# Weight products grouped by high and low parts, and block 2's merges laid out by tokens

## The chip, the cores and the metric

The kernel runs on one core of a Trainium2 chip. A core has a matrix engine, TensorE (PE in the profile, with its weight loads shown apart as PEld), a vector engine (DVE), a scalar engine (ACT), GpSimd (POOL) and SyncE (SP), which issues the transfers from HBM. Each engine works through its own queue in order, and semaphores tie the queues together. TensorE writes into PSUM, and ACT and DVE read it from there. The metric is the device time of the core in microseconds, the median of several executions.

## What is computed

Two blocks of two layers each over 256 tokens of width 1024, all in float32. A layer of block 1 mixes three branches: an mLSTM (a recurrence with gates, run forwards and backwards), a differential attention and a Fourier mix. A layer of block 2 mixes two attentions and ends in a wide MLP. Cut to what the change touches:

```
# block 1, gates of the recurrence: running sums b, running maxima, decays
b = jnp.cumsum(fc, axis=-1)
inter = b + m_st[..., None]
m_row = jnp.maximum(jnp.max(dmat, axis=-1), inter)
a = jnp.exp(dmat - m_row[..., None]) * jnp.einsum('bhtd,bhsd->bhts', qc, kc)

# block 2, one layer
proj = h @ w_in
q_a, k_a, v_a, q_b, k_b, v_b, gate_a, gate_b = jnp.split(proj, IN_OFFSETS, axis=-1)
y_a = swa_attention(q_a, k_a, v_a, sinks) @ w_o_swa
y_b = moba_attention(q_b, k_b, v_b) @ w_o_moba
mixed = jax.nn.sigmoid(gate_a) * y_a + jax.nn.sigmoid(gate_b) * y_b
x = x + gt1[:, None, :] * (mixed @ w_out)
u = jnp.square(jax.nn.relu(rms_adaln(x) @ w_up))
x = x + gt2[:, None, :] * (u @ w_down)
```

## The kernel before

**Products in three parts.** Every large product is made of three. A weight tile of 128 x 1024 comes from HBM (SP's queue, tile name w or a slot s), ACT copies it rounded into its high part (`nc.scalar.activation(h, self.raw[i], AF.Copy)` in `split`), and DVE subtracts that from the tile for the low part. The activations have a high and a low part too (h and hl, or slots). For each piece of the contraction the program makes high x high, high activations x low weights, and low activations x high weights, all added up in one PSUM bank (tiles mm).

**The stream.** `Stream.execute` (L500 on) walks through a list of gemms. A gemm of contraction 1024 has four weight tiles, numbered q = 0 to 3, each with two contraction pieces of 128 by 512 columns (kq is 2). A gemm has several outputs o. In `tok` form an output is 128 tokens by 512 features: the activations are the stationary operand and 512 weight columns move (names `mm<-w,h`). In `feat` form an output is 128 features by the tokens: the weights are stationary and the tokens move, 256 of them in block 2 (names `mm<-h,w`, 128x256). The outer loop is over q, the next over o, then over the two pieces, then over the three products; with `head` or `tail` set, the first or last tiles go output by output. `tile` (L478) hands out a tile only when both parts are planned. The first product of a tile needs its high part; the low part is needed by the second product in `tok` form and by the third in `feat` form, and PE's queue stands still until it is there.

**The order of the rest.** All other work (norms, attention, gates, evacuations) is written as generators that a `Planner` advances. It keeps a running estimate of when each engine is free. After every three products `execute` issues transfers, up to six side steps whose inputs should be there (`plan.side`), and then one `split`: the low part of the oldest tile that has a high part, or else the next high part. Nine buffers of 128 x 1024 hold raw tiles, high parts and low parts, and at most three tiles are split at a time. So the order in each engine's queue is fixed when the program is built; on the chip an engine waits where the estimate was off.

**The gates of the recurrence.** `mlstm_gates` (L1069) runs once in each layer of block 1. On rows 0 to 3 and 32 to 35 it makes the running sums and maxima, then copies the chunk ends one by one into TG, forms the maxima M and the offsets off between chunks, and with 8 and 12 small DVE instructions on 4 x 128 elements (`nc.vector.tensor_scalar(rk[k][rr, cs], R0[rr, cs], off[rr, k, j:j + 1], None, ALU.add)`) the maxima cm and three shifted copies r1, r2, r3. Five small transposes for each of four chunks turn the rows into the columns `cols`.

**Block 2's merges.** In `layer2` (L2145) four gemms in `feat` form give the two gates (`ev_g` puts tanh into tg), and four shorter ones, of contraction 512 and so of two tiles each (wo2), give the two attention outputs. `ev_o` multiplies and adds on DVE, and rounds the sum into the high and low parts yf, which already stand with features on the partitions, as the next gemm (wout2) needs them as its stationary operand. `tneed` makes wout2 wait for the eight pieces of yf one by one.

Of the kernel before, what the change touches and what calls it, by code (L numbers as in the profile page):

```python
# [11 lines left out]
ALU = mybir.AluOpType  # L12
# [37 lines left out]
NSIDE, SLACK, MAXEV, LATE = 6, 1200.0, 4, 400  # L50
NP, NJ, MP = 3, 5, 2
# [284 lines left out]
class Stream:  # L336
# [64 lines left out]
    def build_seq(self):  # L401
# [29 lines left out]
        self.nd = self.ns = self.nl = self.pairs = 0  # L431
# [20 lines left out]
    def split(self, force=False):  # L452
# [5 lines left out]
        if self.nl < self.ns:  # L458
            i = self.gidx[self.nl]
            if force or plan.gate([self.h[i]]) <= plan.t[PE]:  # L460
# [5 lines left out]
                return True  # L466
        if self.ns < len(self.gidx) and self.pairs < (NP + MP if self.more else NP) and len(self.free) > 1 + self.ns - self.nl:
# [10 lines left out]
    def tile(self, i):  # L478

        plan = self.plan  # L480
        while i not in self.l:
# [10 lines left out]
        late = plan.gate([self.h[i], self.l[i]])  # L492
# [5 lines left out]
        return self.h[i], self.l[i]  # L498

    def execute(self):  # L500
        plan, nc = self.plan, self.nc
        self.build_seq()
        nout, evs = 0, []
# [15 lines left out]
        for st in self.prog:  # L519
# [14 lines left out]
            left = [no] * nq  # L534
            ps, seen = [None] * no, [0] * no
            for q, o in visits:
# [7 lines left out]
                h, l = self.tile(i)  # L544
# [6 lines left out]
                for j in range(kq):  # L551
                    kt = q * kq + j
                    s = slice(j * st["width"], (j + 1) * st["width"])
                    for m, (L, R, O) in enumerate(outs[o](h[:, s], l[:, s], kt, ps[o])):
                        nc.tensor.matmul(O, L, R, start=(kt == 0 and m == 0), stop=(seen[o] == st["nkt"] - 1 and m == 2))
                    seen[o] += 1
                    if j == kq - 1:
                        left[q] -= 1
                        if not left[q]:
                            self.drop(self.h.pop(i))  # L560
                            self.drop(self.l.pop(i))
                            self.pairs -= 1
                            if self.joint and self.joint[0] == i:
                                self.joint.pop(0)
                        if seen[o] == st["nkt"]:
                            evac(st["cb"], o, ps[o])
                    self.dma()
                    n = 0
                    while n < NSIDE and plan.side():
                        n += 1  # L570
                    self.split()
# [11 lines left out]
def _build(tc, a, out, es):  # L583
# [377 lines left out]
    def tok(act, t, c0=0, c1=512):  # L961
        ts = slice(128 * t, 128 * t + 128)

        def f(h, l, kt, ps):
            H, L = act(kt)
            O = ps[:, 0:c1 - c0]
            return [(H[:, ts], h[:, c0:c1], O), (H[:, ts], l[:, c0:c1], O), (L[:, ts], h[:, c0:c1], O)]
        return f

    def feat(view, f0, n):  # L970
        fs = slice(128 * f0, 128 * f0 + 128)

        def f(h, l, kt, ps):
# [4 lines left out]
            return [(h[:, fs], H, O), (h[:, fs], L, O), (l[:, fs], H, O)]  # L978
# [90 lines left out]
    def mlstm_gates(rowt, l, res):  # L1069

        def gen(lane):
            pre, lf, b, v, cm, r1, r2, r3 = (rowt[:, i, :] for i in range(8))
            R = slice(0, 36)
            nc.gpsimd.memset(rowt[R, 2, :], 0.0)
            nc.gpsimd.memset(rowt[R, 4:8, :], 0.0)
# [24 lines left out]
            TG = sm.tile([128, 2, 4], F32, name="TG", tag="TG")  # L1100
            nc.vector.memset(TG, 0.0)
            for i, arr in enumerate((b, cm)):
                fw = arr[0:4].rearrange("p (c n) -> p c n", n=128)[:, :, 127]
                bw = arr[32:36].rearrange("p (c n) -> p c n", n=128)[:, :, 0]
                nc.vector.tensor_copy(TG[0:4, i, 0:2], fw[:, 1:3])
                nc.vector.tensor_copy(TG[0:4, i, 2:4], fw[:, 0:4:3])
                for p, j in POS_B.items():
                    nc.vector.tensor_copy(TG[32:36, i, j:j + 1], bw[:, p:p + 1])
            M = sm.tile([128, 4], F32, name="M", tag="M")
            nc.vector.memset(M, 0.0)  # L1110
            for j in range(3):
                nc.vector.tensor_tensor(M[R, j + 1:j + 2], M[R, j:j + 1], TG[R, 1, j:j + 1], ALU.max)
                nc.vector.tensor_tensor(M[R, j + 1:j + 2], M[R, j + 1:j + 2], TG[R, 0, j:j + 1], ALU.add)
            off = sm.tile([128, 4, 4], F32, name="off", tag="off")
            nc.vector.tensor_copy(off[R, 1, 1:4], TG[R, 0, 0:3])
            nc.vector.tensor_tensor(off[R, 2, 2:4], off[R, 1, 2:4], TG[R, 0, 0:2], ALU.add)
            nc.vector.tensor_tensor(off[R, 3, 3:4], off[R, 2, 3:4], TG[R, 0, 0:1], ALU.add)
            yield [DVE]
            dirs = ((slice(0, 4), POS_F), (slice(32, 36), POS_B))
            for rr, pos in dirs:  # L1120
# [1365 lines left out]
```

## Time and profile before

| | |
|---|---|
| median of 3 runs | 2247.6 us (2247.15 to 2248.94) |
| profiled execution, its own time | 2247.62 us |
| its span on the profile | 2245.5 us |
| PE busy | 2200.1 us, 98% |
| DVE busy | 1485.1 us, 66% |
| ACT busy | 1104.3 us, 49% |
| DVE on the low parts of w (451 instructions) | 551.5 us |
| ACT on the high parts of w (459 instructions) | 485.1 us |
| granted TensorE clock | 0.997 over the span |

Almost every instruction is issued through one helper (L318), so groups are told apart by their tiles and not by line. A busy PE is not a PE at its peak: a matmul's record lasts longer than the distance to the next one, because matmuls overlap. What a product costs is read from the distance between starts.

### The profile page before, as it was taken

How to read it: one execution, taken by the hardware profiler on the slowest of the kernel's cores; microseconds unless marked ns; L12 is line 12 of the kernel's file. 1: busy time of each engine (PE TensorE's matmuls, PEld its weight loads, DVE VectorE, ACT ScalarE, POOL GpSimd, SP SyncE). 2: the span in 40 equal slices, each digit the busy share in tenths (PEclk: the TensorE clock that was granted, in tenths of full speed). 3: DMA queues.
4: the chain of work that ended last, by engine and by line, in shares of the span. 5: the costliest groups of instructions: out<-in, count | busy, mean ns of one | idle time of the engine just before them, and what ended most of it. 6: DMA issues, size and time to landing. Idle time of an engine off the chain costs nothing. (4 is left out here: it accounts for less than half of the span.)

```text
span 2245.5 us, 33046 instructions
## 1 busy us (share of the span) xinstructions
PE 2200.1 (98%) x12312; PEld 1821.8 (81%) x12312; DVE 1485.1 (66%) x2778; ACT 1104.3 (49%) x2110; POOL 272.6 (12%) x467
## 2 busy tenths in 40 slices
PE   8999999999999999999999999999999999999999
PEld 6877888877777877877778888787898987798987
DVE  4667745457676744687886788677766656758554
ACT  4345422235565522344543466555855645666653
POOL 1013000014121000110200142003000002100000
PEclk9999999999999999999999999999999999999999
DMA  7443344353322453365675423464354564345454
GB/s 297 144 157 109 121 167 140 132 170 118 103 98 96 140 179 131 140 206 187 233 246 185 158 83 135 157 213 151 123 195 165 180 215 160 132 145 203 160 188 150
DMA packets 99905, 359.73 MB, mean 160 GB/s; under 512 B 11960, under 2 KB 12272, under 8 KB 99744
## 3 DMA queue, kind: packets, MB, share of 16 engines
q1 hardware_dynamic: 96192, 348.34, 45.3%
q0 software_dynamic: 3552, 9.28, 1.5%
q8 instruction: 97, 1.59, 0.3%
q14 instruction: 64, 0.52, 0.1%
HBM read 354.37 MB, written 3.20 MB: 159 GB/s over the span
## 5 line engine op out<-in xcount | busy, mean ns | idle before, releaser
L318 DVE TENSOR_TENSOR w<-w,w 128x1024 fp32r<-128x1024 f32 x451 | 551.5, 1223 | 394.0 <-ACT w L318 340.0
L318 ACT ACTIVATE w<-w 128x1024 fp32r<-128x1024 f32 x459 | 485.1, 1058 | 647.6 <-PE mm L318 595.4
L318 PE MATMUL mm<-h,w 128*128 128x256 f32 (+1 forms) x3280 | 665.5, 326 | 2.8 <-DVE w L318 2.3
L318 PE MATMUL mm<-w,h 128*128 128x512 f32 (+1 forms) x1972 | 597.7, 394 | 12.2 <-DVE w L318 9.0
L318 PEld LDWEIGHTS mm<-h,w 128*128 128x128 f32 x3280 | 479.6, 190 | 57.3 <-issue 9.6
L318 PEld LDWEIGHTS mm<-w,h 128*128 128x128 f32 x1972 | 357.2, 190 | 101.4 <-DVE w L318 15.5
L318 PE MATMUL mm<-w,s 128*128 128x512 f32 x1280 | 309.1, 392 | 1.2 <-DVE w L318 1.1
L318 PE MATMUL mm<-w,hl 128*128 128x512 f32 (+1 forms) x800 | 306.7, 383 | 0.0
L318 PEld LDWEIGHTS mm<-w,s 128*128 128x128 f32 x1280 | 238.4, 188 | 52.6 <-DVE w L318 3.2
L318 PE MATMUL mm<-hl,w 128*128 128x512 f32 (+1 forms) x656 | 245.8, 375 | 0.0
L318 PE MATMUL mm<-s,w 128*128 128x512 f32 (+1 forms) x960 | 182.2, 349 | 0.0
L318 PEld LDWEIGHTS mm<-w,hl 128*128 128x128 f32 x800 | 150.8, 189 | 29.9 <-DVE hl L318 0.2
L318 PEld LDWEIGHTS mm<-s,w 128*128 128x128 f32 x960 | 153.1, 190 | 23.5 <-issue 2.0
L318 DVE SCALAR_TENSOR_TENSOR acc<-w,stat,acc 128x512 f32<-128x512 f32 x192 | 143.8, 749 | 42.3 <-DMA w<-in_wada_dram 35.5
L318 PEld LDWEIGHTS mm<-hl,w 128*128 128x128 f32 x656 | 124.0, 189 | 18.7 <-issue 1.0
L318 ACT ACTIVATE s<-mm 128x512 f32<-128x512 f32 (+2 forms) x126 | 65.2, 521 | 62.8 <-PE mm L318 62.8
L318 POOL TENSOR_TENSOR qrs<-qrs,mhalf 128x8 f32<-128x8 f32 (+2 forms) x48 | 77.1, 1607 | 4.0
L318 PE MATMUL p<-s 64*128 64x256 f32 (+3 forms) x464 | 75.4, 389 | 1.4 <-DVE s L318 0.7
L318 POOL TENSOR_SCALAR ls<-ls 128x1 f32<-128x1 f32 x72 | 29.8, 414 | 344.5 <-ACT l1a L318 127.1
L318 PE MATMUL mm<-s,s 128*128 128x512 f32 x256 | 68.7, 390 | 0.0
L318 DVE TENSOR_REDUCE ls<-p 128x1 f32<-128x512 f32 (+1 forms) x96 | 52.8, 595 | 12.7 <-PE p L318 12.3
L318 ACT ACTIVATE s<-w 128x1024 fp32r<-128x1024 f32 x43 | 45.5, 1058 | 27.7 <-PE mm L318 21.0
(348 smaller groups left out, 2399.3 us busy)
## 6 DMA issues: line engine op xcount, KB each, us to landing
w<-in_win_dram SPq DMA_DIRECT2D x272, 512.0 KB, 3.3
w<-in_wada_dram SPq DMA_DIRECT2D x144, 512.0 KB, 3.5
w<-in_wmix_dram SPq DMA_DIRECT2D x64, 512.0 KB, 3.3
w<-in_wup_dram SPq DMA_DIRECT2D x64, 512.0 KB, 3.4
w<-in_wdn_dram SPq DMA_DIRECT2D x64, 512.0 KB, 3.2
w<-in_wo_dram SPq DMA_DIRECT2D x16, 512.0 KB, 3.2
w<-in_wout_dram SPq DMA_DIRECT2D x16, 512.0 KB, 3.5
s<-in_x_dram SPq DMA_DIRECT2D x4, 512.0 KB, 7.3
```

Of the source, the lines that this page charges most:

```text
L318: r = f(*a, **k)
```

## The change

**Products by parts.** In `tok` and `feat` the three products are handed out as part 0 (high x high), part 1 (low activations x high weights) and part 2 (high activations x low weights). For the inner tiles of a gemm (neither the first nor the last, with two pieces in the tile) `execute` goes through all outputs with part 0, then all with part 1, then all with part 2. The first tile of a gemm goes output by output in the order 0, 2, 1, the last one output by output in the order 0, 1, 2. The low part of a tile is asked for only ahead of part 2.

**High parts ahead.** `split` prefers the next high part to a pending low one while fewer than AHEAD = 2 tiles past the current one have theirs, and `pump`, called after every three products, may make one split ahead of the side steps as well as one behind them.

**Gates as products.** In `mlstm_gates` the chunk ends are copied four at a time, one instruction makes the maxima, and the shifted copies are gone: two products with 36 rows, one with the rows and a repeated identity and one with ones and a block of offsets on the diagonal, give all four shifts in PSUM. One small transpose is left.

**Block 2 by tokens.** The gate gemms and the wo2 gemms go from `feat` to `tok` form. `ev_o` then works on 128 tokens by 512 features, and `turned` transposes the sum back, four 128 x 128 transposes for each of the two halves of the tokens and of the features, and makes yf's high part (ACT) and low part (DVE) out of PSUM.

**Exponentials.** In the attentions of block 2 each pair of exponentials waits for the planner's ACT (`yield [ACT]`).

```diff
 NSIDE, SLACK, MAXEV, LATE = 6, 1200.0, 4, 400
+AHEAD = 2
...
-        self.nd = self.ns = self.nl = self.pairs = 0
+        self.nd = self.ns = self.nl = self.pairs = self.cur = 0
+        self.rank = {i: k for k, i in enumerate(self.gidx)}
...
-        if self.nl < self.ns:
+        if self.nl < self.ns and not (self.ns < self.cur + AHEAD and self.split_high(force)):
             i = self.gidx[self.nl]
...
+    def high(self, i):
+
+        return self.tile(i, False)[0]
...
+    def pump(self):
+
+        self.dma()
+        if self.ns < self.cur + AHEAD:
+            self.split()
+        n = 0
+        while n < NSIDE and self.plan.side():
+            n += 1
+        self.split()
...
-            visits = [(q, o) for o in range(no) for q in range(hd)]
-            visits += [(q, o) for q in range(hd, nq - tl) for o in range(no)]
-            visits += [(q, o) for o in range(no) for q in range(nq - tl, nq)]
...
+            early, late = (0, 2, 1), (0, 1, 2)
+            steps = [(q, o, early) for o in range(no) for q in range(hd)]
+            for q in range(hd, nq - tl):
+                if 0 < q < nq - 1 and kq == 2:
+                    steps += [(q, o, (p,)) for p in late for o in range(no)]
+                else:
+                    steps += [(q, o, late if q else early) for o in range(no)]
+            steps += [(q, o, late) for o in range(no) for q in range(nq - tl, nq)]
...
-                h, l = self.tile(i)
+                self.cur = max(self.cur, self.rank[i])
+                h = self.high(i)
...
-                for j in range(kq):
-                    kt = q * kq + j
-                    s = slice(j * st["width"], (j + 1) * st["width"])
-                    for m, (L, R, O) in enumerate(outs[o](h[:, s], l[:, s], kt, ps[o])):
-                        nc.tensor.matmul(O, L, R, start=(kt == 0 and m == 0), stop=(seen[o] == st["nkt"] - 1 and m == 2))
...
+                for p in parts:
+                    l = self.tile(i)[1] if p == 2 else None
+                    for j in range(kq):
+                        kt = q * kq + j
+                        s = slice(j * st["width"], (j + 1) * st["width"])
+                        L, R, O = outs[o](h[:, s], None if l is None else l[:, s], kt, ps[o])[p]
+                        nc.tensor.matmul(O, L, R, start=(seen[o] == 0), stop=(seen[o] == total - 1))
+                        seen[o] += 1
+                        since += 1
+                        if since >= 3 and seen[o] < total:
+                            since = 0
+                            self.pump()
...
-            return [(H[:, ts], h[:, c0:c1], O), (H[:, ts], l[:, c0:c1], O), (L[:, ts], h[:, c0:c1], O)]
+            return [(H[:, ts], h[:, c0:c1], O), (L[:, ts], h[:, c0:c1], O), l is not None and (H[:, ts], l[:, c0:c1], O)]
...
-            for i, arr in enumerate((b, cm)):
-                fw = arr[0:4].rearrange("p (c n) -> p c n", n=128)[:, :, 127]
...
-                for p, j in POS_B.items():
-                    nc.vector.tensor_copy(TG[32:36, i, j:j + 1], bw[:, p:p + 1])
...
+            nc.vector.tensor_copy(MP[f_, 1:3, :], by(f_, slice(0, 2)))
...
-            for rr, pos in dirs:
-                for p, j in pos.items():
-                    cs = slice(128 * p, 128 * p + 128)
-                    nc.vector.tensor_scalar(cm[rr, cs], cm[rr, cs], M[rr, j:j + 1], None, ALU.max)
...
+            nc.vector.tensor_tensor(cm4, cm4, MP[R, :, 0:1].to_broadcast([36, 4, 128]), ALU.max)
...
-                        if j >= k:
-                            cs = slice(128 * p, 128 * p + 128)
-                            nc.vector.tensor_scalar(rk[k][rr, cs], R0[rr, cs], off[rr, k, j:j + 1], None, ALU.add)
+            for c in range(4):
+                nc.vector.tensor_tensor(off[:, c], ident[R, R].unsqueeze(1).to_broadcast([36, 4, 36]),
+                                        MP[R, c, 1:5].unsqueeze(2).to_broadcast([36, 4, 36]), ALU.mult)
...
-                for i, arr in enumerate((R0, r1, r2, r3, F)):
-                    nc.tensor.transpose(ps[:, 36 * i:36 * i + 36], arr[R, 128 * p:128 * p + 128], ident[R, R])
...
+                nc.tensor.matmul(pk, R0[R, cs], ident[R, R].unsqueeze(1).to_broadcast([36, 4, 36]), start=True, stop=False)
+                nc.tensor.matmul(pk, ones[R], off[:, p], start=False, stop=True)
+                nc.tensor.transpose(ps[:, 144:180], F[R, cs], ident[R, R])
...
-                            yield []
+                            yield [ACT]
...
-                gemm(lambda q, kind=kind, c=c: win[l, 4 + 2 * kind + c, q], 8, 512,
-                     lambda: [feat(act, f, 256) for f in range(4)], ev_g, pre=pre_g if kind + c == 0 else None)
+                gemm(lambda q, kind=kind, c=c: win[l, 4 + 2 * kind + c, q], 8, 512, toks, ev_g,
+                     pre=pre_g if kind + c == 0 else None)
...
+        def turned(t, c, src):
+
+            def gen(_):
+                pt = yield Bank(src)
+                transposes(pt, src, 4)
+                yield [pt]
+                H, L = (y[:, 4 * c:4 * c + 4, 128 * t:128 * t + 128] for y in st["yf"])
+                pv = pt.rearrange("p (k n) -> p k n", k=4)
+                nc.scalar.activation(H, pv, AF.Copy, scale=0.5)
+                yield [H]
+                nc.vector.scalar_tensor_tensor(L, pv, 0.5, H.bitcast(F32), ALU.mult, ALU.subtract)
+                plan.release(pt)
+                for kt in range(4 * c, 4 * c + 4):
+                    fin(f"yfm{l}-{kt}")
+            plan.add("yfT", gen, kind="pri")
...
                     if kind:
                         yield [FREE, t]
-                        nc.vector.tensor_tensor(t, st["tg"][:, 0, kt, :], t, ALU.add)
...
+                        nc.vector.tensor_tensor(t, st["tg"][:, 0, i, cs], t, ALU.add)
+                        turned(i, c, t)
                 gemm(lambda q, kind=kind, c=c: a["wo2"][l, kind, c, q], 4, 512,
-                     lambda ov=ov: [feat(ov, f, 256) for f in range(4)], ev_o,
+                     lambda ov=ov: [tok(ov, t) for t in range(2)], ev_o,
                      need=(f"att{kind}",) if c == 0 else ())
```

PE, block 1's second layer, a `tok` gemm with four outputs, at the third tile (q is 2; mm names the bank of an output, h and hl are the high and low activations, the first w is the tile's high part and the second its low part). Before:

```order
L318 MATMUL mm_8889<-w4_8854,hl_7968 128x512
L318 MATMUL mm_8856<-w2_8907,h_7967 128x512
L318 MATMUL mm_8856<-w8_8944,h_7967 128x512
L318 MATMUL mm_8856<-w2_8907,hl_7968 128x512
...
L318 MATMUL p2_8963<-cst_80,s3_8624 128x36 x5
L318 MATMUL mm_8869<-w2_8907,h_7967 128x512
L318 MATMUL mm_8869<-w8_8944,h_7967 128x512
L318 MATMUL mm_8869<-w2_8907,hl_7968 128x512
L318 MATMUL p3_8978<-cst_80,s3_8624 128x36 x5
```

The same place now:

```order
L319 MATMUL mm_8810<-w7_8863,h_7936 128x512 x2
L319 MATMUL mm_8827<-w7_8863,h_7936 128x512
L319 MATMUL p2_8922<-cst_80,s3_8592 128x144
L319 MATMUL p2_8922<-s3_8592,one_84 128x144
L319 MATMUL p2_8922<-cst_80,s3_8592 128x36
...
L319 MATMUL mm_8849<-w7_8863,h_7936 128x512 x2
L319 MATMUL mm_8810<-w7_8863,hl_7937 128x512 x2
L319 MATMUL mm_8827<-w7_8863,hl_7937 128x512 x2
L319 MATMUL mm_8835<-w7_8863,hl_7937 128x512 x2
L319 MATMUL mm_8849<-w7_8863,hl_7937 128x512 x2
L319 MATMUL mm_8810<-w2_8893,h_7936 128x512 x2
```

The low part (w8_8944, now w2_8893) stood one product behind the tile's first and stands sixteen behind it now.

PE, block 2's first layer, the last wo2 gemm and the start of wout2 (s4 holds the attention outputs, s0 is yf, s5 is tg). Before:

```order
L318 MATMUL mm_15398<-s4_14140,w4_15356 128x256
...
L318 MATMUL mm_15410<-s4_14140,w3_15341 128x256 x2
L318 MATMUL mm_15410<-s4_14140,w4_15356 128x256
...
L318 MATMUL mm_15461<-w6_15375,s0_14423 128x512
L318 MATMUL mm_15461<-w8_15396,s0_14423 128x512
```

Now:

```order
L319 MATMUL mm_15038<-w2_15003,s4_14077 128x512 x4
L319 MATMUL mm_15038<-w0_15008,s4_14077 128x512 x2
L319 MATMUL mm_15082<-w4_15019,s0_14358 128x512 x2
...
L319 MATMUL p0_15100<-cst_80,s5_14357 128x128 x4
...
L319 MATMUL mm_15082<-w1_15058,s0_14358 128x512 x2
L319 MATMUL p1_15123<-cst_80,s5_14357 128x128 x4
L319 MATMUL mm_15094<-w1_15058,s0_14358 128x512 x2
...
L319 MATMUL mm_15082<-w0_15076,s0_14358 128x512 x2
```

The products are 512 wide instead of 256, and the transposes of the second half of yf stand inside wout2's first two tiles, ahead of its third, which needs them.

DVE, the gates of block 1's second layer (s3 holds their rows). Before:

```order
L318 COPY TG_8825<-s3_8624 4x2 x2
L318 COPY TG_8825<-s3_8624 4x1 x4
...
L318 TENSOR_SCALAR s3_8624<-s3_8624,M_8839 4x128 x8
L318 TENSOR_TENSOR s3_8624<-s3_8624 36x512
L318 TENSOR_SCALAR s3_8624<-s3_8624 36x512
L318 TENSOR_SCALAR s3_8624<-s3_8624,off_8847 4x128 x12
```

Now:

```order
L319 COPY s3_8592<-s3_8592 4x2x2 x4
...
L319 COPY s3_8592<-s3_8592 4x10
L319 COPY s3_8592<-s3_8592 4x2x5 x3
L319 TENSOR_TENSOR s3_8592<-s3_8592 36x512 x2
L319 TENSOR_SCALAR s3_8592<-s3_8592 36x512
L319 TENSOR_TENSOR s3_8592<-cst_80,s3_8592 36x144 x4
```

Twenty instructions on 4 x 128 elements went, one on 36 x 512 and four on 36 x 144 came.

## Rows read from the trace of the kernel before

**Rows 1.** The page: span, engines (busy us, share, instructions), clock in 40 slices.
```profile
span 2245.5 us, 33046 instructions
...
PE 2200.1 (98%) x12312; PEld 1821.8 (81%) x12312; DVE 1485.1 (66%) x2778; ACT 1104.3 (49%) x2110; POOL 272.6 (12%) x467
...
PEclk9999999999999999999999999999999999999999
```

**Rows 2.** Waits of PE: who waited for whom, us in total, times, longest.
```profile
PE mm L318 <- DVE w L318: 12.4, 14, 1.6
...
PE mm L318 <- DVE h L318: 2.7, 4, 1.0
```

**Rows 3.** Timeline of PE (start us, us, instruction, count): unbroken runs of products.
```profile
2159.71 12.63 PE L318 MATMUL mm<-w,s 128*128 128x512 f32 x55
...
2084.45 7.72 PE L318 MATMUL mm<-h,w 128*128 128x256 f32 x63
...
1650.11 6.16 PE L318 MATMUL mm<-s,w 128*128 128x256 f32 x50
```

**Rows 4.** Timeline, all engines: four transposes, and products behind small work and inside a run.
```profile
1937.66 0.63 PE L318 MATMUL p<-cst,qr 128*128 128x128 f32 x4 [1.36 <-DVE qr L318]
...
1938.05 0.47 PE L318 MATMUL mm<-w,h 128*128 128x512 f32 x1
...
487.50 0.71 PE L318 MATMUL mm<-w,h 128*128 128x512 f32 x2
...
488.27 0.63 PE L318 MATMUL mm<-w,h 128*128 128x512 f32 x2
```

**Rows 5.** Timeline of PE and DVE around the gates, and a wider float32 product.
```profile
97.45 0.50 PE L318 MATMUL p<-cst,s 36*128 36x36 f32 x5
97.88 0.50 PE L318 MATMUL mm<-h,w 128*128 128x512 f32 x1
...
1114.76 1.99 PE L318 MATMUL p<-s,l1b 128*128 128x256 f32 x8 [0.97 <-ACT l1b L318]
...
1013.36 1.87 DVE L318 TENSOR_SCALAR s<-s,M 4x128 f32<-4x128 f32 x8
...
1016.40 2.90 DVE L318 TENSOR_SCALAR s<-s,off 4x128 f32<-4x128 f32 x12
```

**Rows 6.** Timeline of PE: products that waited for a low part (idle before, releaser).
```profile
31.67 0.50 PE L318 MATMUL mm<-w,h 128*128 128x512 f32 x1 [0.43 <-DVE w L318]
...
1019.31 0.39 PE L318 MATMUL mm<-w,h 128*128 128x512 f32 x1
...
1021.27 0.50 PE L318 MATMUL mm<-w,h 128*128 128x512 f32 x1 [1.58 <-DVE w L318]
...
1061.34 0.50 PE L318 MATMUL mm<-w,h 128*128 128x512 f32 x1 [0.56 <-DVE w L318]
...
1091.68 0.50 PE L318 MATMUL mm<-w,h 128*128 128x512 f32 x1 [0.86 <-DVE w L318]
...
1890.41 1.66 PE L318 MATMUL mm<-w,h 128*128 128x512 f32 x6 [0.59 <-DVE w L318]
...
1940.04 7.13 PE L318 MATMUL mm<-w,h 128*128 128x512 f32 x23 [1.51 <-DVE w L318]
...
1948.31 1.94 PE L318 MATMUL mm<-h,w 128*128 128x256 f32 x14 [0.47 <-DVE w L318]
...
1975.98 2.89 PE L318 MATMUL mm<-h,w 128*128 128x256 f32 x22 [1.02 <-DVE w L318]
```

**Rows 7.** Busy us of each engine in stretches of 50 us, then clock, DMA share, GB/s.
```profile
1050.00:1100.00 50.00, 48.48 (x223) 36.40 (x222) 41.61 (x81) 32.44 (x73) 10.38 (x19) 1.00 0.63 220
...
1900.00:1950.00 50.00, 46.65 (x243) 37.51 (x243) 40.09 (x70) 30.35 (x66) 14.58 (x18) 0.97 0.41 143
```

**Rows 8.** Groups of DVE and ACT by form: busy us, mean ns, idle before.
```profile
L318 DVE TENSOR_TENSOR w<-w,w 128x1024 fp32r<-128x1024 f32 x451 | 551.5, 1223 | 394.0 <-ACT w L318 340.0
...
L318 DVE SCALAR_TENSOR_TENSOR s<-s,mm 128x512 f32<-128x512 f32 x36 | 24.1, 681 | 2.4 <-PE mm L318 2.4
...
L318 ACT ACTIVATE s<-p 128x512 fp32r<-128x512 f32 x36 | 21.4, 595 | 19.4 <-PE p L318 19.1
```

More of the change, by code (lines that the diff above doesn't have):

```diff
@@ L476, in split, with tile @@
         return False
-    def tile(self, i):
+    def high(self, i):
+        return self.tile(i, False)[0]
+    def tile(self, i, low=True):
         plan = self.plan
-        while i not in self.l:
+        while i not in (self.l if low else self.h):
             self.dma()
@@ L491, in tile @@
                 plan.side(force=True)
-        late = plan.gate([self.h[i], self.l[i]])
+        late = plan.gate([self.h[i], self.l[i]] if low else [self.h[i]])
         while late > plan.t[PE] + LATE:
@@ L502, in execute @@
         self.build_seq()
-        nout, evs = 0, []
+        nout, evs, since = 0, [], 0
         def evac(cb, o, ps):
@@ L530, in execute @@
             hd, tl = st["head"], st["tail"]
-            visits = [(q, o) for o in range(no) for q in range(hd)]
-            visits += [(q, o) for q in range(hd, nq - tl) for o in range(no)]
-            visits += [(q, o) for o in range(no) for q in range(nq - tl, nq)]
-            left = [no] * nq
-            ps, seen = [None] * no, [0] * no
-            for q, o in visits:
+            early, late = (0, 2, 1), (0, 1, 2)
[6 more added lines that the diff above has]
+            steps += [(q, o, late) for o in range(no) for q in range(nq - tl, nq)]
+            left = [3 * no] * nq
+            ps, seen, total = [None] * no, [0] * no, 3 * st["nkt"]
+            for q, o, parts in steps:
                 if st["tneed"]:
@@ L550, in execute @@
                     nout += 1
-                for j in range(kq):
-                    kt = q * kq + j
-                    s = slice(j * st["width"], (j + 1) * st["width"])
-                    for m, (L, R, O) in enumerate(outs[o](h[:, s], l[:, s], kt, ps[o])):
-                        nc.tensor.matmul(O, L, R, start=(kt == 0 and m == 0), stop=(seen[o] == st["nkt"] - 1 and m == 2))
[L556 to L571, printed above, removed]
+                for p in parts:
[10 more added lines that the diff above has]
+                            self.pump()
+                    left[q] -= 1
+                    if not left[q]:
+                        self.drop(self.h.pop(i))
+                        self.drop(self.l.pop(i))
+                        self.pairs -= 1
+                        if self.joint and self.joint[0] == i:
+                            self.joint.pop(0)
+                if seen[o] == total:
+                    evac(st["cb"], o, ps[o])
+                    since = 0
+                    self.pump()
         plan.drain("ev")
@@ L977, in f @@
                 O = O.rearrange("p (t c) -> p t c", c=128)
-            return [(h[:, fs], H, O), (h[:, fs], L, O), (l[:, fs], H, O)]
+            return [(h[:, fs], H, O), (h[:, fs], L, O), l is not None and (l[:, fs], H, O)]
         return f
@@ L1071, in gen @@
         def gen(lane):
-            pre, lf, b, v, cm, r1, r2, r3 = (rowt[:, i, :] for i in range(8))
+            pre, lf, b, v, cm, r1 = (rowt[:, i, :] for i in range(6))
             R = slice(0, 36)
             nc.gpsimd.memset(rowt[R, 2, :], 0.0)
-            nc.gpsimd.memset(rowt[R, 4:8, :], 0.0)
+            nc.gpsimd.memset(rowt[R, 4, :], 0.0)
             nc.scalar.activation(lf[R], pre[64:100], AF.Abs)
@@ L1109, in gen @@
-            M = sm.tile([128, 4], F32, name="M", tag="M")
-            nc.vector.memset(M, 0.0)
-            for j in range(3):
[L1112 to L1116, printed above, removed]
@@ L1117, in gen @@
[L1117 to L1123 removed]
+            TG, MO, MP = (rowt[:, 7, 128 + o:128 + o + n] for o, n in ((0, 8), (8, 20), (28, 20)))
@@ L1124, in gen @@
+            nc.vector.tensor_tensor(cm4, cm4, MP[R, :, 0:1].to_broadcast([36, 4, 128]), ALU.max)
+            yield [DVE]
             F = lf
@@ L1468, in g_out @@
             H, L = act(kt)
-            return [(h, H, ps), (h, L, ps), (lo, H, ps)]
+            return [(h, H, ps), (h, L, ps), lo is not None and (lo, H, ps)]
         def ev_q(f, ps):
```

60 lines of the change are left out of this document (35 added, 25 removed).

## The prediction

> **What bounds the kernel now.** I read the engines' shares first. PE is busy for 98% of the span at the full clock, DVE for 66%, ACT for 49% [rows 1], so the time is PE's queue: its products at their price, plus the places where it stands still. The price comes from the distance between starts. Fifty-five products of 512 columns take 12.63 us with a tail of 0.39, so (12.63 - 0.39) / 54 = 0.227 us each; sixty-three of 256 columns take (7.72 - 0.28) / 62 = 0.120, and fifty in the wo2 gemms the same 0.120 [rows 3]. The program has 6480 of the wide kind and 3072 of the narrow: 1471 + 369 = 1840 us. The rest is small work on PE and waits. The waits that the change aims at are one line: products that waited for a low part from DVE, 12.4 us in 14 places [rows 2]. That is the idle time behind a modelled end. By starts a place costs a little more: 1021.27 - 1019.31 = 1.96 us where 0.227 is due, so 1.73 and not 1.58 [rows 6]. With 0.15 more each the 14 places cost 14.5 us.
>
> The profiled execution took 2247.6 us, 2.1 outside its span, and that is also the median of the runs; the sum is made against 2247.6. About 0.2% (4.5 us) is what a measurement of this kernel can tell from no change.
>
> **Wider products.** Going from `feat` to `tok` turns 1152 products of 256 columns into 576 of 512 (counted in the order of each): 1152 x 0.120 = 138.2 us become 576 x 0.227 = 130.8 [rows 3]. That is 7.5 us less, all on PE. [...]
>
> **Transposes of yf.** Eight runs of four transposes are new. One such run takes 1937.66 to 1938.05, 0.39 us [rows 4], and the product behind it comes late: two products after small work take 0.71 us, inside a run 0.63 [rows 4]. So 0.39 to 0.48 each, 3.1 to 3.8 us; I take 3.5.
>
> **Gates as products.** Five transposes take PE 0.43 us up to the next product's start [rows 5], eight times. Now three instructions stand there: two products of 36 rows by 144 columns in float32, and one transpose. No row shows such a product. Below it stands the small transpose, some 0.07 us; above it a 256-column float32 product, 1.99 us for eight records, which are four products, so (1.99 - 0.38) / 4 = 0.4 at least and 0.43 by the starts [rows 5]. By its width, 144/256, I take 0.24: 2 x 0.24 + 0.07 + 0.09 for the restart = 0.64 against 0.43, so 1.7 us more in all (-1.0 to +4.7). On DVE the 20 small instructions, 1.87 + 2.90 us in each layer [rows 5], become one of about 0.68 and four of some 0.2; I count no time for that by itself, since PE's one wait behind them (at 1021.27) is counted below.
>
> **More interruptions.** In the order PE leaves its stream of large products 387 times before and 416 times now. Eight of the 29 are the transposes. The others cost the late product, 0.09 us: 1.9 (0 to 2.9).
>
> These four come to -7.5 + 3.5 + 1.7 + 1.9 = -0.4 us. The structure is a wash; the change lives from the waits.
>
> **Low parts that came late.** I placed the 14 waits by the order of the products. Seven stand at inner tiles, 7.2 us idle or 8.3 by starts (the first at 31.67, the last at 1975.98 [rows 6]). There the low part is now needed behind 16 products with four outputs and behind 8 with two, against one or two before: seven products more are 7 x 0.227 = 1.59 us. The longest in block 2, 1.51 + 0.15, keeps 0.07; the others vanish: 8.2 us. Five stand at the first tile of a gemm (the first at 1061.34, the last at 1948.31 [rows 6]; 3.7 idle, 4.5 by starts): there the low part still comes second, behind two products instead of one, so 0.2 each, 1.1 us. Two stand in a gemm's last tile (1091.68, three products more, 0.7) or a gemm that goes output by output (1890.41, 0.2). Together 10.2 us. What may be late next is the low part of the following tile: in nine stretches of 50 us DVE is busy for over 40 (41.61 in the first that I show, 40.09 in the last [rows 7]), and a low part is 1.22 us of it [rows 8]. With four outputs a tile lasts 24 x 0.227 = 5.4 us and the delay is caught up; with two it lasts 2.7. So I take 8.0 of the 10.2 (2 to 14.5).
>
> **The clock.** In 1900 to 1950 the granted clock is 0.97 [rows 7]: 1.5 us of it lost to a spell at 1.2 GHz instead of 2.4, entered behind two waits, 1.36 us for qr and 1.51 for a low part [rows 4, 6]. Without the second I count it as gone: -1.5 (to 0).
>
> **Low activations.** Four waits for low activations, 2.7 us [rows 2], are in gemms that start output by output. Part 1 comes last there now, behind four products instead of two; a norm's chain sets the end, so I take 0.5 (0 to 1.5).
>
> **From wo2 to wout2.** yf was ready with the last outputs; now a sum, four transposes, a copy and a low part stand behind the last product: DVE 0.68 twice, PE 0.44 behind at most 0.68 of products, ACT 0.60, DVE 0.68 [rows 4, 8], 3.8 us, with DVE also on the other half's (0.68 x 3) and two weight tiles' low parts (2.4): up to 8.2. wout2's first two tiles give 24 x 0.227 = 5.4 us of cover, and its third needs the low part 0.9 later. So 0 to 2.3 us in each layer; I take 0.5 twice, +1.0.
>
> **Edits at nothing.** Evacuations of 512 columns (0.68 on DVE [rows 8]) replace two of 256 on engines with room. Exponentials held for the planner's ACT let other copies through; the wait for qr (1.36 [rows 4]) bounds that either way. No transfer is added; a raw tile stays until its later low part is made, but transfers run at 0.4 to 0.6 of the time of their engines [rows 7].
>
> **Sum.** -0.4 - 8.0 - 1.5 - 0.5 + 1.0 = -9.4: 2238.2 us.
>
> **The rivals.** *The waits move.* In two-output gemms DVE is the slower partner; what inner tiles save comes back at the last tile and the next first one, and the clock drop stays. Then 2 us of the waits are won: -0.4 - 2.0 + 1.0 = -1.4, 2246. For it: DVE's 40 and more of 50 us. Against: the waits are 14 single places, and the plain runs of rows 3 show no steady shortage. *First tiles starve (slower).* A pending low part now steps behind the next high part, and the first tile of each gemm needs its low part after two products, 0.45 us. In the nine busy stretches, 450 us, some 40 gemms of 11 us start. If DVE takes one operation more ahead (0.68 to 1.22 [rows 8]) at half of them, 20 x 1.0 us are added: 2238.2 + 20 = 2258. It decides from nine such first tiles on. Against: DVE's queue is in program order, and the five waits there now average under 1 us. *More goes than the low parts.* First tiles are served too (the other 6.5 of the 14.5), chains of attention shift by the held exponentials (1.4) and the small terms fall at their low ends (-5.4 instead of -0.4): down to about 2225; a middle of it is 2228. *Banks.* Outputs now alternate every two products. In the run of 55 they alternate every six and the step costs nothing measurable, 0.227 throughout at the full clock [rows 1, 3]; if ten more drops like that of rows 7 came, 15 us: 2253. The Trainium skill (TensorE: Matmul & The Clock Gate, section on the second failure mode, PSUM-queue cycling) warns that cycling through banks can make the clock swing; no row here shows it.
>
> **How the numbers follow.** Forecast 2231 to 2243: 0.58. More goes, below 2231: 0.14. The waits move, 2243 to 2252: 0.17. First tiles starve: 0.09. Banks: 0.02. So faster by over 0.2% 0.72, within 0.2% 0.17, slower 0.11. The low ends of all terms give 2225, the high ends about 2254; the range that leaves out no more than 2 in 10 is 2227 to 2251.
>
> **What would show it.** Right: PE's wait for DVE w falls from 12.4 to under 6 us and what is left stands at first tiles; 1152 fewer narrow products at 0.120; clock 1.00 in the stretch of the second layer's attention; no wait between wo2 and wout2 above 1 us. Wrong: a wait for DVE w as long as before with other places, waits for yf at wout2's third tile, or float32 products in the gates above 0.43 us.

## The result and the profile after

The changed kernel takes 2231.1 us (median of four runs, 2228.6 to 2236.2) against 2247.4 for the kernel before (2246.0 to 2248.9). The ratio is 0.993, with a 95% interval of 0.9911 to 0.995: 16.3 us less. The forecast was 2238.2, range 2227 to 2251, faster with 0.72. The sign and the range hold; the gain is 7 us larger than the sum of -9.4 said.

The page of the kernel after (busy us, share of the span, instructions) answers [rows 1]:

```profile
span 2228.1 us, 31863 instructions
...
PE 2195.4 (99%) x11768; PEld 1793.2 (80%) x11768; DVE 1477.5 (66%) x2706; ACT 1101.9 (49%) x2086; POOL 263.7 (12%) x465
```

The work of PE, DVE and ACT is as it was, within 8 us each. PE's waits (us in total, times, longest) answer [rows 2]:

```profile
PE mm L319 <- DVE w L319: 4.9, 7, 1.2
PE mm L319 <- ACT h L319: 4.2, 4, 1.7
...
PE mm L319 <- DVE s L319: 2.5, 3, 1.2
PE p L319 <- DVE s L319: 1.9, 3, 1.4
PE p L319 <- ACT l1a L319: 1.8, 1, 1.8
...
PE mm L319 <- DVE h L319: 0.4, 2, 0.2
```

Products wait for a low part in one of the buffers w for 4.9 us instead of 12.4. Some 40 of the 502 low parts of weights lie in a slot instead (name s), and there the wait grew from 0.7 to 2.5. For activations, products waited 2.7 us for high parts (ACT h) and 2.7 for low parts (DVE h) before; it is 4.2 and 0.4 now. The two rows of before that [rows 2] do not show:

```profile
PE mm L318 <- ACT h L318: 2.7, 3, 1.2
...
PE mm L318 <- DVE s L318: 0.7, 2, 0.4
```

Idle time stands behind a modelled end, so I also did the account by starts. From one start on PE to the next, the price of the first instruction is taken away (0.227 or 0.120 us for a large product, the usual distance for small ones). What is 0.15 us or more is a late start. With the order of the program beside the trace, each of the 502 roundings on ACT and 502 subtractions on DVE is paired with the first product that reads its result, so a late start that ends as a low part arrives is known as one. "First tile" is a gemm's first, for low parts in a buffer w; those in a slot have a column of their own. The products' other late starts hold the waits for activations, part of what the half clock costs and, in e1, e5 and e9, eight roundings that came late; the last column is all prices and the lateness below 0.15 us. The 6.0 us ahead of PE's first start and behind its last are the same in all and left out. Late starts in us / places, for the two kernels and for five of the experiments below:

| kernel | low part, first tiles | low part, other tiles | low part in a slot | small work on PE | other late products | start | all else |
|---|---|---|---|---|---|---|---|
| before | 5.3 / 6 | 12.0 / 14 | 1.6 / 4 | 24.1 / 51 | 27.6 | 8.0 | 2160.8 |
| after | 3.3 / 4 | 2.9 / 4 | 3.3 / 4 | 19.2 / 51 | 27.0 | 6.1 | 2160.2 |
| e1, grouped and ahead | 2.9 / 4 | 1.5 / 3 | 3.4 / 4 | 17.6 / 47 | 28.5 | 7.2 | 2160.9 |
| e9, grouped, not ahead | 4.7 / 6 | 9.5 / 9 | 8.9 / 9 | 32.3 / 67 | 26.0 | 6.6 | 2166.3 |
| e5, after, not ahead | 2.5 / 4 | 6.7 / 9 | 8.9 / 9 | 29.3 / 66 | 23.1 | 7.4 | 2164.4 |
| e11, ahead, not grouped | 2.0 / 5 | 9.4 / 19 | 3.4 / 4 | 30.5 / 58 | 27.9 | 6.1 | 2166.4 |
| e6, after, not grouped | 1.7 / 3 | 14.1 / 24 | 3.4 / 4 | 28.3 / 56 | 31.0 | 6.5 | 2165.1 |

From before to after that is -2.0 - 9.1 + 1.7 - 4.9 - 0.6 - 1.9 - 0.6 = -17.4, the difference of the two spans. All late low parts together fall from 18.9 us to 9.6.

### The profile page after: what moved, and what is told of

It reads as the page before. It is cut to its first block, busy times and chain, and to the rows that moved or that the text cites. A ratio compares the mean times of both kernels' runs of the same rounds, so it can differ in the third digit from the quotient of the medians.

```text
span 2228.1 us, 31863 instructions
## 1 busy us (share of the span) xinstructions
PE 2195.4 (99%) x11768; PEld 1793.2 (80%) x11768; DVE 1477.5 (66%) x2706; ACT 1101.9 (49%) x2086; POOL 263.7 (12%) x465
## 5 line engine op out<-in xcount | busy, mean ns | idle before, releaser
L319 PEld LDWEIGHTS mm<-w,h 128*128 128x128 f32 x2404 | 432.0, 189 | 108.6 <-issue 13.4
L319 PE MATMUL mm<-h,w 128*128 128x256 f32 (+1 forms) x2496 | 481.5, 336 | 0.3 <-DVE w L319 0.3
L319 PEld LDWEIGHTS mm<-h,w 128*128 128x128 f32 x2496 | 374.2, 190 | 46.2 <-issue 5.0
L319 PEld LDWEIGHTS mm<-w,s 128*128 128x128 f32 x1460 | 272.4, 188 | 59.2 <-ACT s L319 1.6
L319 PE MATMUL mm<-w,hl 128*128 128x512 f32 (+1 forms) x800 | 234.9, 389 | 0.0
L319 PE MATMUL mm<-hl,w 128*128 128x512 f32 (+1 forms) x656 | 183.9, 383 | 0.0
L319 PE MATMUL mm<-s,w 128*128 128x512 f32 x576 | 135.6, 392 | 0.0
L319 PEld LDWEIGHTS mm<-s,w 128*128 128x128 f32 x576 | 106.9, 188 | 23.5 <-issue 1.6
L319 POOL TENSOR_SCALAR ls<-ls 128x1 f32<-128x1 f32 x72 | 29.3, 406 | 350.4 <-ACT l0a L319 103.5
L319 ACT ACTIVATE s<-p 128x512 fp32r<-128x512 f32 (+3 forms) x76 | 40.4, 535 | 55.3 <-PE p L319 55.3
L319 PEld LDWEIGHTS p<-s 64*128 64x128 f32 (+1 forms) x464 | 41.6, 187 | 24.6 <-issue 13.1
```

The source lines that it names most:

```text
L319: r = f(*a, **k)
```

## The experiments

Each kernel ran beside the kernel before on the same chip. A ratio is to the runs of before in that session, with its 95% interval. Diffs are cut to their core.

**One part alone, on the kernel before.** e1 takes over `execute`, `split`, `tile`, `high`, `pump` and the three parts of `tok` and `feat`: the order by parts with the high parts ahead. The other three each take one part of the rest.

e1:

```diff
-                h, l = self.tile(i)
+                self.cur = max(self.cur, self.rank[i])
+                h = self.high(i)
...
+        if self.ns < self.cur + AHEAD:
+            self.split()
...
+                if 0 < q < nq - 1 and kq == 2:
+                    steps += [(q, o, (p,)) for p in late for o in range(no)]
```

> Only the grouping by parts with high parts ahead, the rest as before. Theory: this part removes the waits for late low parts (14.5 us by starts before, some 6 left after) and the clock drop at 1940, and changes no product: 2247.4 - 8 to -12 = 2235 to 2239, PE's wait for DVE w under 6 us. Rival (the gain comes from the re-planned order, not from the grouping): within 4 us of before.

e2:

```diff
-                     lambda: [feat(act, f, 256) for f in range(4)], ev_g, pre=pre_g if kind + c == 0 else None)
+                gemm(lambda q, kind=kind, c=c: win[l, 4 + 2 * kind + c, q], 8, 512, toks, ev_g,
...
-                     lambda ov=ov: [feat(ov, f, 256) for f in range(4)], ev_o,
+                     lambda ov=ov: [tok(ov, t) for t in range(2)], ev_o,
```

> Only block 2's gates and merges by tokens. Theory: 1152 x 0.120 - 576 x 0.227 = -7.5, 32 transposes and restarts +4.2, hand-over to wout2 0 to +2: -3.3 to -1.3, so 2244 to 2246, with the waits for low parts as before. Rival (this part carries the gain): under 2240.

e3:

```diff
-                for i, arr in enumerate((R0, r1, r2, r3, F)):
...
+                nc.tensor.matmul(pk, ones[R], off[:, p], start=False, stop=True)
+                nc.tensor.transpose(ps[:, 144:180], F[R, cs], ident[R, R])
```

> Only the recurrent gates as products. Theory: PE pays 0.2 us more at eight places, DVE does 5 us less work: +1.7 from products, less up to 1.7 if the wait at 1021 goes: 2247 to 2249. Rival (DVE's relief frees PE): under 2244.

e4:

```diff
-                            yield []
+                            yield [ACT]
```

> Only the exponentials of block 2's attentions held for the planner's ACT. Theory: no product changes and no path is known that it shortens: 2246 to 2249. Rival (the 10 us won in block 2's second layer come from here, since in that stretch ACT's queue set the waits): under 2242, with the waits between 1930 and 1990 gone.

| kernel | median us | ratio to before | profiled span |
|---|---|---|---|
| e1, grouped with high parts ahead | 2230.7 | 0.9927 (0.9900 to 0.9954) | 2228.0 |
| e2, tokens in block 2 | 2248.7 | 1.0005 (0.9994 to 1.0017) | 2243.0 |
| e3, gates as products | 2245.6 | 0.9993 (0.9983 to 1.0004) | 2246.1 |
| e4, exponentials held | 2247.6 | 0.9996 (0.9983 to 1.0009) | 2241.1 |

The gain is e1's alone, to within what can be measured, and the other three move nothing. Only e4 lies in the range that I expected: e1 is 4 us below its range, e3 1.4 below, e2 2.7 above. PE's waits for low parts, first of e1 and then of e2, show it too (us, times, longest):

```profile
PE mm L319 <- DVE w L319: 2.9, 5, 1.0
```

```profile
PE mm L318 <- DVE w L318: 14.5, 17, 2.0
```

By starts, e2 has 2.1 us less than before in all else, where the wider products show, and 3.1 more in late low parts (22.0 in 28 places against 18.9 in 24).

**Which half of e1?** e5 is the kernel after without the preference for high parts; e6 keeps that and gives up the order by parts.

e5:

```diff
-AHEAD = 2
+AHEAD = 0
```

> The changed kernel with AHEAD = 0: products grouped, but the low part of the oldest tile is again made ahead of the next high part, and pump makes one split at its end. Theory (the order of the products gives the cover): within 4 us of the changed kernel, 2228 to 2235. Rival (high parts made ahead are what counts): 2238 or more, with new waits of PE for ACT's high parts.

e6:

```diff
-                if 0 < q < nq - 1 and kq == 2:
-                    steps += [(q, o, (p,)) for p in late for o in range(no)]
-                else:
-                    steps += [(q, o, late if q else early) for o in range(no)]
-            steps += [(q, o, late) for o in range(no) for q in range(nq - tl, nq)]
+                steps += [(q, o, early) for o in range(no)]
+            steps += [(q, o, early) for o in range(no) for q in range(nq - tl, nq)]
```

> The changed kernel with no tile grouped: every tile goes output by output, high x high, then the low weights, then the low activations; high parts are still made ahead. Theory: the low weights are needed behind two products again, so PE's waits for DVE w come back to 8 us and more: 2238 to 2246. Rival (high parts ahead carry the gain): 2228 to 2234.

e5 took 2252.7 us, ratio 1.003 (1.0016 to 1.0044), and e6 2258.4, ratio 1.0057 (1.0042 to 1.0072). My theory, that the order of the products gives the cover and the rest little, fell: each half without the other is slower than the kernel before.

**Other forms of the same.** e7 leaves each gemm's first tile output by output but asks for its low part last, except in gemms that go output by output over several tiles at their head, whose order stays; e8 changes only the planner's allowance, which makes it plan the same program anew.

e7:

```diff
-                    steps += [(q, o, late if q else early) for o in range(no)]
+                    steps += [(q, o, late) for o in range(no)]
```

> The changed kernel with the first tile of a gemm in the order 0, 1, 2 as the last one: its low part is needed behind four products of an output instead of two. Theory (the waits that are left stand at first tiles): the waits for DVE w fall from 4.9 to 2 to 4 us, 2228 to 2231. Rival (low activations are the later ones at a gemm's start): new waits for DVE h or s, 2231 to 2236.

e8:

```diff
-NSIDE, SLACK, MAXEV, LATE = 6, 1200.0, 4, 400
+NSIDE, SLACK, MAXEV, LATE = 6, 1250.0, 4, 400
```

> The changed kernel with SLACK 1250 instead of 1200, a null change that makes the planner place side work a little differently. It shows how much of a difference is only the order that came out: theory, within 3 us of the changed kernel (2228 to 2234). Rival (a chance order gave most of the 16 us): 2238 or more.

e7 took 2236.7 us (2234.7 to 2247.8), ratio 0.9961 (0.9946 to 0.9976). That is above both ranges. Its late first tiles fell from four to two and kept their 3.4 us: one at 1405 waited 2.05 although two products more stood ahead. So the last 3 us at first tiles are no matter of two products more. The profiled execution of e7 is 4.8 us longer than that of the kernel after, and 3.4 of that is the clock: it runs at half (1.2 GHz) for 10.2 us inside the program, the kernel after for 3.4. e8 took 2233.0 us (2229.5 to 2241.0), ratio 0.994 (0.9923 to 0.9956); its longest execution is at half clock for 20.5 us inside the program. A difference of 2 or 3 us between two variants may be the planner's and says nothing of their edits.

**Both halves again, on the kernel before.** e9 is e1 with AHEAD = 0. e10 is e9 with the old rule that a tile is handed out only when both parts are planned. e11 is e1 with e6's loop. e12 is e1 with the gates as products.

e9, against e1:

```diff
-AHEAD = 2
+AHEAD = 0
```

> Grouping alone on the kernel before (block 2 and the gates as before), with AHEAD = 0. It repeats the earlier run without high parts ahead on another order of the side work. Theory (late high parts and late low parts are the two halves of one trade, so grouping without high parts ahead loses): 2246 to 2254 again. Rival (that run only met a bad order): 2230 to 2238.

e10, against e9:

```diff
-                h = self.high(i)
+                h = self.tile(i)[0]
```

> As the run above, but a tile is handed out only when both its parts are planned, as in the kernel before: so the planner asks and places as before, and only the order of the products inside a tile differs. Theory (seven to fifteen products of cover let late low parts arrive unseen): PE's wait for DVE w falls from 12.4 to under 7 us and the time to 2236 to 2241. Rival (cover alone is worth little, the planner uses it up): 2243 to 2248.

e11, against e1:

```diff
-                if 0 < q < nq - 1 and kq == 2:
-                    steps += [(q, o, (p,)) for p in late for o in range(no)]
...
+                steps += [(q, o, early) for o in range(no)]
```

> High parts ahead on the kernel before, no tile grouped. It repeats the earlier run of high parts ahead alone on another order of the side work. Theory (high parts ahead put the low parts behind them, and without cover PE waits for them): 2248 to 2258 with waits for DVE w of 10 us or more. Rival (a bad order): 2230 to 2240.

e12, against e1:

```diff
-                for i, arr in enumerate((R0, r1, r2, r3, F)):
...
+                nc.tensor.matmul(pk, ones[R], off[:, p], start=False, stop=True)
```

> The changed kernel without block 2 by tokens and without the held exponentials: grouping, high parts ahead and the gates as products. Theory (the grouping carries the gain and the rest adds nothing): within 3 us of grouping alone, 2228 to 2233. Rival (the tokens in block 2 carry a few us on top of the grouping): 2234 or more.

| kernel | median us | ratio to before |
|---|---|---|
| e9, grouped, not ahead | 2260.1 | 1.0062 (1.0047 to 1.0077) |
| e10, and handed out whole | 2257.4 | 1.0054 (1.0039 to 1.0069) |
| e11, ahead, not grouped | 2255.6 | 1.0046 (1.0030 to 1.0063) |
| e12, grouped, ahead, gates | 2232.0 | 0.9943 (0.9928 to 0.9957) |

e9 and e11 repeat e5 and e6 without block 2's tokens, the gates and the held exponentials, so the loss belongs to the halves. e10 met neither what I expected nor its rival: when a tile is handed out does not decide it, and its late low parts still cost 17.9 us. e9 and e6 lost more than I expected, by 6 and 12 us; in e11 the wait for DVE w is 6.1 us and not 10 or more. e12 adds nothing to e1.

What each half lacks can be read. **Grouped, not ahead:** with a low part pending, no next high part is made. The low part is then needed 8 or 16 products later, but both parts are made late. On PE's timeline of e9, in the second layer of block 2 (start us, us, instruction, count, idle before and its releaser):

```profile
1899.86 1.19 PE L319 MATMUL mm<-w,h 128*128 128x512 f32 x4 [0.92 <-DVE w L319]
1903.20 1.66 PE L319 MATMUL mm<-s,h 128*128 128x512 f32 x6 [1.70 <-DVE s L319]
...
1907.58 0.74 PE L319 MATMUL mm<-w,h 128*128 128x512 f32 x2 [0.45 <-ACT w L319]
1908.84 2.58 PE L319 MATMUL mm<-w,h 128*128 128x512 f32 x10 [0.52 <-DVE w L319]
...
1958.57 2.11 PE L319 MATMUL mm<-w,h 128*128 128x512 f32 x8 [1.23 <-DVE w L319]
1961.64 2.11 PE L319 MATMUL mm<-w,h 128*128 128x512 f32 x8 [0.97 <-DVE w L319]
```

At 1903.20 the low part that is late lies in a slot. At 1907.58 and 1908.84 a product waits for the high part from ACT, then the next for the low part of the same tile; that subtraction began 0.03 us after the rounding. At 1958.57 the low part comes after eight products of cover, at 1961.64 after four. The kernel after does this layer some 25 us earlier, and from 1866 to 1990 its products have two waits, one for a gemm's first high activations and one for a low part:

```profile
1874.30 1.95 PE L319 MATMUL mm<-w,h 128*128 128x512 f32 x6 [1.65 <-ACT h L319]
...
1933.28 1.89 PE L319 MATMUL mm<-w,h 128*128 128x512 f32 x7 [0.34 <-DVE w L319]
```

**Ahead, not grouped:** the next high part goes first, and the low part, still needed behind two products, is later by that. In e11 19 tiles behind a gemm's first are late. Ten of them are in the wide MLP gemms, 0.27 or 0.28 us each, where before had no late tile; that time hardly shows as idle, since it lies under the modelled end of the product ahead.

**Together:** the low parts that are ready less than 1 us ahead of their product fall from 206 of 502 before to 44 after. Ahead alone (e11) leaves 141. Grouping alone (e9) leaves 58, but 24 of those come late, against 11 of 45 in e1. PE's waits for low parts in e9 are longer than before, in the buffers and in the slots together 18.7 us against 13.1:

```profile
PE mm L319 <- DVE w L319: 11.6, 14, 1.9
PE mm L319 <- DVE s L319: 7.1, 7, 1.7
```

Low parts explain only a part of the losses, though. Against before, all late low parts cost 4.2 us more in e9 and 0.2 in e6, and 0.9 less in e5 and 4.1 in e11. The largest part is the half clock. Inside the program (behind its first 30 us and ahead of its last 10) the trace's clock is at half for 3.4 us in before and in after and never in e1, but for 23.9 us in e9, 17.1 in e6 and 13.7 in e5 and in e11. At half a microsecond lost for each, that is 10, 7, 5 and 5 us more than before, where the profiled executions are 14.8, 10.6, 2.8 and 6.2 us longer. Every execution of these four has a mean clock of 0.993 to 0.997; e1's have 0.998 or 0.999. Beside the clock and, in e9, the low parts stands small work on PE that comes late: its column has +4 to +8 us, but of e9's 8.2 about 7 lie in its spells at half clock, and of e11's 6.4 about 2.5. PE's waits for small work in e11, in the same attention:

```profile
1943.13 0.63 PE L319 MATMUL p<-cst,qr 128*128 128x128 f32 x4 [2.57 <-DVE qr L319]
1945.78 1.09 PE L319 MATMUL p<-cst,qr 128*128 128x128 f32 x4 [2.03 <-DVE ls L319]
```

Here the norm's chain on DVE (qr, ls) is behind, and PE stands at its transposes for 4.6 us; before, this place cost 1.36 [rows 4]. And the half clock follows such waits: in e11 a spell of 3.4 us begins at 1945. Windows of 1300 to 1350 (us, busy us of PE, PEld, DVE, ACT and POOL, granted clock, DMA share, GB/s), of the kernel after and then of e9:

```profile
1300.00:1350.00 50.00, 47.85 (x308) 40.57 (x307) 39.11 (x86) 31.21 (x71) 19.30 (x31) 0.97 0.30 96
```

```profile
1300.00:1350.00 50.00, 46.23 (x276) 38.21 (x275) 33.12 (x74) 27.97 (x66) 12.95 (x25) 0.83 0.22 77
```

The 0.83 of e9 is 17 us at 1.2 GHz instead of 2.4, entered at the waits of 1.40 us for l0b and 1.11 for vb, both from ACT: 0.17 x 50 = 8.5 us lost. The two longest spells of e6, 6.8 us each, show as 0.93:

```profile
1570.00:1620.00 50.00, 44.47 (x238) 33.69 (x236) 36.42 (x65) 34.25 (x80) 4.98 (x4) 0.93 0.35 111
1930.00:1980.00 50.00, 44.54 (x249) 33.78 (x248) 36.73 (x66) 31.25 (x73) 4.98 (x4) 0.93 0.37 116
```

Why the planner puts these chains later when it has only one of the two halves is not settled. The trace shows that they are late, not which of its estimates moved them.

## Why the prediction was right, and where it was short

**The structure: right.** Forecast -0.4, measured -0.6 ("all else" in the table). Wider products: in the kernel after, PE's timeline has unbroken runs of both widths.

```profile
2067.05 23.20 PE L319 MATMUL mm<-h,w 128*128 128x256 f32 x192
...
2136.16 86.10 PE L319 MATMUL mm<-w,s 128*128 128x512 f32 x379
```

(86.10 - 0.39) / 378 = 0.227 us, (23.20 - 0.28) / 191 = 0.120: the prices of [rows 3], in runs three to seven times as long. The -7.5 follows. The transposes of yf, in the first layer's wout2:

```profile
1659.61 0.60 PE L319 MATMUL p<-cst,s 128*128 128x128 f32 x4
1659.96 0.93 PE L319 MATMUL mm<-w,s 128*128 128x512 f32 x3
1660.73 0.60 PE L319 MATMUL p<-cst,s 128*128 128x128 f32 x4
```

Four take 0.35 us, and the three products behind them 0.77 instead of 0.68: 0.44 for a run, inside the 0.39 to 0.48. The gates:

```profile
93.18 0.51 PE L319 MATMUL p<-cst,s 36*128 36x144 f32 x2
93.53 0.41 PE L319 MATMUL p<-s,one 36*128 36x144 f32 x2
93.78 0.19 PE L319 MATMUL p<-cst,s 36*128 36x36 f32 x1
93.90 0.42 PE L319 MATMUL p<-acc,one 128*32 128x128 f32 x8
```

From 93.18 to 93.90 is 0.72 us where [rows 5] had 0.43. The two float32 products (two records each) take 0.35 and 0.25, 0.30 on average where I took 0.24 by the width: the second bears that out, the first, right behind a large product, takes 0.1 more. So +2.3 in all and not +1.7.

**Low parts: right in mechanism, short by 1 us.** Forecast -8.0, measured -9.3 (18.9 to 9.6). I counted 14 places at 14.5 us. The pairing finds 15.4 us at those and 1.9 more in six short ones that hide under the modelled end. Behind the first tiles 12.0 us became 2.9, so the delay of the following tile, for which I took 2.2 off, did not come there. It came in the slots, whose row of waits the sum left out: 1.6 us became 3.3, in gemms that go output by output at their head and ask for the low part behind two products. At first tiles my forecast for all five was -1.1, and 5.3 became 3.3. So the sign that I had set, under 6 us in the row of DVE w, held with 4.9; that what is left stands at first tiles is true of four in twelve. The longest waits that are left:

```profile
1271.66 0.51 PE L319 MATMUL mm<-w,h 128*128 128x512 f32 x1 [1.23 <-DVE w L319]
...
1579.17 2.12 PE L319 MATMUL mm<-w,h 128*128 128x512 f32 x8 [1.09 <-DVE w L319]
...
1691.83 0.74 PE L319 MATMUL mm<-s,h 128*128 128x512 f32 x2 [1.20 <-DVE s L319]
...
2043.48 0.73 PE L319 MATMUL mm<-s,h 128*128 128x512 f32 x2 [1.20 <-DVE s L319]
```

**What gives the cover: wrong.** I worked the gain out from the order of the products alone (seven products more are 1.59 us) and saw the preference for high parts only as a danger, in the rival of starving first tiles. e5 and e9 show that without it the grouped order loses 6 and 14 us. The rival's half is right as well: the preference alone loses, 10 us in e11, but in small work and at the half clock, not at first tiles (2.0 us late there, 5.3 before).

**Small work on PE: the term that was missing.** 24.1 us of late starts became 19.2 (17.6 in e1), and in the sum this was nothing. I read rows of waits for products and treated transposes and scores in the attentions as fixed, though they share DVE and ACT with the low parts. It is the largest part of the 7 us that the forecast lacks; the low parts add 1.3, and the start of the program 1.9. What makes the small work earlier is argued and not shown.

**The clock: half right.** The spell at 1940 went: from 1900 to 1950 the granted clock is 1.00 where [rows 7] have 0.97.

```profile
1900.00:1950.00 50.00, 49.66 (x261) 39.34 (x261) 42.57 (x67) 33.20 (x68) 11.44 (x10) 1.00 0.51 159
```

PE is busy for 49.66 of these 50 us, 46.65 before, with DVE busier than before. But a spell of the same length came at 1317, behind a wait that was not there: the 1.78 us for l1a in

```profile
1315.31 0.96 PE L319 MATMUL p<-s 64*128 64x512 f32 x5 [1.78 <-ACT l1a L319]
```

So 3.4 us at half the clock went at one place and came at another, and nothing is won. At the start of the program the spell was 3.4 us instead of 6.8, which is most of the -1.9 there; e1 to e4 have 3.4 to 6.8 at that place, so I put it down to chance.

**Low activations: the sum came out, the term did not.** Forecast -0.5. The waits for low activations fell from 2.7 us to 0.4, more than the 1.5 that the range allowed. But those for high activations, which the sum had at nothing, grew from 2.7 to 4.2, so -0.8 is left. The two longest are 1.65 us each and stand at a gemm's first product, as at 1521.60:

```profile
1521.60 3.29 PE L319 MATMUL mm<-w,h 128*128 128x512 f32 x12 [1.65 <-ACT h L319]
```

**From wo2 to wout2: too careful.** Forecast +1.0, measured 0. (By its own figures the upper end for a layer was 8.2 - 5.4 - 0.9 = 1.9 us and not 2.3.) The last transposes of yf stand at 1669.17 in the first layer, and fourteen products follow without a wait:

```profile
1669.17 0.60 PE L319 MATMUL p<-cst,s 128*128 128x128 f32 x4
1669.52 3.45 PE L319 MATMUL mm<-w,s 128*128 128x512 f32 x14
```

**A wait that I had put at nothing.** The products of the gates now wait for DVE in block 1's second layer:

```profile
1017.11 0.48 PE L319 MATMUL p<-cst,s 36*128 36x144 f32 x2 [1.42 <-DVE s L319]
```

The low part that PE waited 1.58 us for at 1021.27 [rows 6] is in time, and 1.42 went to the gates at almost the same place. e1 has neither the gates nor this wait, but there a product starts 1.4 us late at 1018 for a tile's high part. Of the rivals, three did not come: the waits did not move to the gemms' ends as a whole (a gain of 1.4 was priced for that; the slots took back 1.7), first tiles did not starve, and outputs that alternate every two products run at the price of before. The fourth, that more goes than the low parts (below 2231), came in part: the measured 2231.1 stands at its border. Small work did come earlier, but with e1 and not with the held exponentials that this rival named.

## What to carry to other kernels

To get an operand out of the way of a queue took two things at once in this kernel: work that does not need it yet, and the next tile's first operand made ahead. Each alone lost 6 to 14 us and both together won 16, so test such a pair as a pair before dropping either half. In a program whose order a planner fixes, price also the small work that shares the producing engine: it moved by -5 us with the pair, half as much as the waits that were aimed at, and by +4 to +8 with one half. And read the granted clock of each variant before explaining its time: with one half alone, 5 to 10 us were the clock's.

## What was not expected of the hardware

A queue that is busy for 98 to 99% of its span still drops to 1.2 GHz for 3.4 us and more behind single waits of 1 to 2 us: in the kernel after behind 1.78 us, in e9 for 17 us behind two waits of 1.40 and 1.11 that lie 1.3 us apart. Not every such wait does it: behind the 1.65 us at 1521.60 and at 1874.30 the granted clock stays at 1.00. Each microsecond of it costs half of one: the 23 products from 1940.04 on [rows 6] start over 7.13 - 0.39 = 6.74 us where 22 x 0.227 = 4.99 are due, 1.75 more in a spell of 3.4. And a float32 product of 36 rows and 144 columns is not cheaper by its rows: the second of a pair takes 0.25 us, against 0.43 for 128 rows and 256 columns [rows 5], which is 0.58 of the time for 0.56 of the columns.
